# Mixing sum of the recurrent projections on GpSimd, value copies on ScalarE, one buffer for two 32-row results

## The chip, the cores and the metric

One core of a Trainium2 chip runs the whole kernel. The metric is the device time of one execution in microseconds (us), the median of several runs. TensorE (PE in the profile) multiplies matrices; VectorE (DVE), ScalarE (ACT) and GpSimd (POOL) do the elementwise work; SyncE (SP) issues the loads and stores. Each engine works through its own instructions strictly in order, and waits where one of them needs something that another engine or a transfer has not finished.

## What is computed

One layer of a hybrid decoder, for 256 prompt tokens and 8 decode tokens, so 264 columns in all:

```python
x = x + 0.5 * swiglu(rmsnorm(x, n1), f1g, f1u, f1d)          # first FFN, width 5504
proj = rmsnorm(x, nm) @ w_in                                 # q, k, v of attention | recurrent columns
xm = proj + mu * (prev - proj)                               # recurrent part: mix with the token before
r, k, v, wl, al, gl = split(xm)                              # 1024 + 1024 + 1024 + 64 + 64 + 128
S, y = wkv_scan(S0, r, logw, k, v, kk, a)                    # RWKV-7 state, 16 heads of 64
mixed = concat(attention, groupnorm(y) * g)
x = x + mixed @ w_out
x = x + 0.5 * swiglu(rmsnorm(x, n2), f2g, f2u, f2d)          # second FFN
y = rmsnorm(x, final)
```

All of it is float32. The change touches the line `xm = ...` and the scan over the prompt, which the kernel computes in chunks of 64 tokens with the inverse of a triangular matrix for each chunk.

## The kernel before

**The weight stream.** Activations lie with the model dimension on the 128 partitions and the 264 tokens along the free axis. Every weight matrix is streamed once, in chunks of 128x512. `chunk` (L116 to L129) loads a chunk into the ring `raw` (6 buffers, SP), rounds it on ScalarE to `hi` (L127, ring of 4), and forms the remainder `lo = raw - hi` on VectorE (L58 through the helper `tt`; some chunks on GpSimd). `gemm` (L133) then multiplies each of the four 128x128 blocks three times, hi by the rounded activation, hi by its remainder and lo by the rounded activation: 12 matmuls a chunk, into the accumulators `acc`. A cast or a subtraction that is late stops TensorE when the chunks ahead of it are used up.

**The mixing stage.** Between the FFNs stand 38 column blocks of w_in (4 chunks each). `win` computes one. `shifted` (L400) handles the 26 recurrent ones: block 0 and 1 are the small inputs `la` and `sgl`, then r, k and v of each of 8 pairs of heads. VectorE scales the accumulator by the norm into `pj` (a ring of three, raised in priority), GpSimd saves the last columns, ScalarE writes the previous token's columns times mu into `d`, and VectorE adds the own columns times `nmu` (that is 1 - mu) with one scalar_tensor_tensor (the helper `stt`, L61).

**The recurrent pairs.** `prep` (L419) makes the decay and key matrices of a pair (with a reciprocal of 128x264 on VectorE, L439). Two pairs form a batch, 4 batches in all. `chain` (L550) works on a batch: it loads the triangular matrices from DRAM into `X` and `Xt` (L562, L563), runs 30 steps of two small VectorE instructions each (`st`, then `Xt`, L569 to L576), sends the result through DRAM into `TT` (L581, L586), transposes the 32x32 blocks on VectorE into `TN` (L591), and multiplies twice on TensorE for the off-diagonal blocks, with a ScalarE copy `zs` between (L610). `TN` uses 32 of each 64 partitions, `zs` the other 32. Then come `pW` and `pU` on TensorE, the copies `W` (L637) and `uv` (L638 on VectorE, L639 on ScalarE), the products with W (pP, pG), those with uv (pN, pY), and the chunk-by-chunk state products.

**What sets the order.** All of these are generators, advanced one step after each weight chunk. The framework's scheduler then places every instruction of each engine by a simulated timeline in which data and buffers are waited for, with `chunk` and `pj` raised in priority. So a change of one instruction's engine can move others.

Of the kernel before, what the change touches and what calls it, by code (L numbers as in the profile page):

```python
# [9 lines left out]
AF = mybir.ActivationFunctionType  # L10
ALU = mybir.AluOpType
AX = mybir.AxisListType

P = 128
NP = 256
NB = 8
T = NP + NB
# [7 lines left out]
HALF = (slice(0, 64), slice(64, 128))  # L25
# [22 lines left out]
def body(tc, I, O):  # L48
    nc = tc.nc
    V, A, G, TE, SP = nc.vector, nc.scalar, nc.gpsimd, nc.tensor, nc.sync  # L50
    cnt = [0]

    def uid(s):
        cnt[0] += 1
        return f"{s}{cnt[0]}"

    def tt(e, out, a, b, op):
        return e.tensor_tensor(out=out, in0=a, in1=b, op=op)  # L58

    def stt(out, a, s, b, op0, op1):  # L60
        return V.scalar_tensor_tensor(out=out, in0=a, scalar=s, in1=b, op0=op0, op1=op1)  # L61
# [5 lines left out]
    def act(out, in_, f, **k):  # L67
        return A.activation(out=out, in_=in_, func=f, **k)  # L68
# [18 lines left out]
    def spawn(g):  # L87
        tasks.append(g)
        return g
# [5 lines left out]
    with ExitStack() as ctx:  # L95
# [17 lines left out]
        def mp():  # L113
            return pp.tile([P, 512], F32, tag="m", bufs=NM, name=uid("m"))
# [49 lines left out]
        def vc(i):  # L164
            return vec[:, i:i + 1]
# [192 lines left out]
        def mixing_body(mx, n2, n3, XD):  # L358
            def fix(shape, name):
                return mx.tile(list(shape), F32, name=name)  # L360

            def ring(shape, tag, bufs):
                return mx.tile(list(shape), F32, tag=tag, bufs=bufs, name=uid(tag))
# [16 lines left out]
            nmu = fix((P, NSH), "nmu")  # L380
# [11 lines left out]
            def win(t):  # L392
                ps = acc()
                gemm(ps, I["win"][t], n2.xs, tick, share=t >= LKV + 4)
                if not have[0]:
                    n2.rstd(rs)
                    have[0] = True
                return ps

            def shifted(t, d):  # L400
                ps = win(t)
                pj = PJ[t % 3]
                with tc.high_priority():
                    tt(V, pj[:, 1:1 + T], ps[:, :T], rs, ALU.mult)
                G.tensor_copy(shc[:, t, :], pj[:, NP:NP + NB + 1])
                act(d[:, :NP], pj[:, 0:NP], AF.Copy, scale=vc(VMU + t))
                A.copy(d[:, NP:], ss[:, t, :])
                stt(d, pj[:, 1:1 + T], nmu[:, t:t + 1], d, ALU.mult, ALU.add)
                return d

            la, sgl = fix((P, T), "la"), fix((P, T), "sgl")
# [138 lines left out]
            def chain(bt):  # L550
                n = bt.n
# [17 lines left out]
                for s in range(1, 31):  # L569
                    m, w = -(-s // ng), 31 - s  # L570
                    t = ring((ng * nr, m, w), "st", 2)
# [5 lines left out]
                for g in range(ng):  # L577
                    d = Y[g * nr:(g + 1) * nr].rearrange("p j t -> p (j t)")
# [10 lines left out]
                TN = ring((P, n * 4, 32), "TN", 1)  # L589
# [3 lines left out]
                def sub(h, x):  # L593
                    return slice(h * 64 + x * 32, h * 64 + x * 32 + 32)

                def quads(k):
                    return slice(k * 4, k * 4 + 4), slice(k * P, k * P + P)

                ps = mp()
                for c in range(4):  # L600
                    for k in range(n):
                        for h in range(2):
                            j = k * 4 + c
                            mm(ps[sub(h, 1 - k), j * 32:j * 32 + 32],
                               bt.Gm[k][h][sub(h, 0), c, 32:64], TN[sub(h, 0), j, :])
                zs = ring((P, n * 4, 32), "zs", 1)
                for k in range(n):
                    c, x = quads(k)
                    for h in range(2):
# [8 lines left out]
                for k in range(n):  # L618
                    c, x = quads(k)
# [4 lines left out]
                uv = bt.UV  # L624
                W, PT = ring((P, n, 3, 64), "W", 1), ring((P, n, 3, 64), "PT", 1)
                N = ring((P, n, 4, 64), "N", 1)
                pW, pU = mp(), mp()
# [7 lines left out]
                                       bt.KR[k][HALF[h], a, c, :])  # L635
                pW, pU = (ps.rearrange("p (k c t) -> p k c t", k=n, c=4) for ps in (pW, pU))
                A.copy(W, pW[:, :, 1:4, :])  # L637
                V.tensor_copy(uv[HALF[0], :, :, HALF[0]].rearrange("p c k t -> p k c t"), pU[HALF[1]])  # L638
                A.copy(uv[HALF[1], :, :, HALF[1]].rearrange("p c k t -> p k c t"), pU[HALF[0]])  # L639
                yield  # L640
                pP, pG = mp(), mp()
                for k in range(n):
# [62 lines left out]
                for k in range(n):  # L705
                    p, o = bt.p0 + k, Ys[k]
# [116 lines left out]
            def dec_attend(p, qs):  # L823
# [44 lines left out]
                for i, q in enumerate(qs):  # L868
                    G.tensor_copy(q[:, NP:T], od[:, i])

            shifted(0, la)
            act(tw[0:64, :], la[0:64, :], AF.Tanh)
            shifted(1, sgl)
            act(sgl, sgl, AF.Sigmoid)
            bat, att, bts, qs = [], [], [], []
            for kind, i in SEQ:
                if kind == "b":
                    bt = newbatch(i)
                    for k in range(BATCH[i]):
                        p = bt.p0 + k  # L880
                        x = [shifted(2 + 3 * p + j, tmp()) for j in range(3)]
                        spawn(prep(p, bt, k, *x))
                    bat.append(spawn(chain(bt)))
                    bts.append(bt)
                    if len(bat) == len(BATCH):
                        A.dma_start(O["sh"], shc)
                elif kind == "kv":
                    w, p = i // 2, i % 2
# [6 lines left out]
                else:  # L895
# [6 lines left out]
                    if i % 4 == 3:  # L902
                        p = i // 4
                        d = spawn(dec_attend(p, qs[4 * p:]))
# [187 lines left out]
```

## Time and profile before

| | us |
|---|---|
| median of 3 runs | 2003.16 |
| the 3 runs | 2001.62, 2003.16, 2003.61 |
| the profiled execution's own time | 2001.57 |
| its span in the profile | 1999.8 |
| busy: TensorE / VectorE / ScalarE / GpSimd | 1969.5 / 1301.4 / 1065.4 / 343.1 |
| VectorE / ScalarE / GpSimd busy in the recurrent part, 690 to 1190 us | 369.2 / 327.3 / 146.1 |

The span runs from the first to the last instruction of the profiled execution; 1.77 us lie around it. Busy time of an engine that nobody waits for costs nothing. A row of the timeline gives the start, the duration, the engine, the line (L58, L61, L68 and L74 are the helpers `tt`, `stt`, `act` and `mm`), the operation, output and input by name, and in brackets the idle time before it with what ended it.

### The profile page before, as it was taken

The page shows a single profiled execution, that of the slowest core. Times are in us where ns is not written, and L with a number is a line of the kernel's source. Part 1 is how long each engine was busy: PE and PEld are TensorE (multiplying, and loading weights), DVE is VectorE, ACT ScalarE, POOL GpSimd, SP SyncE. Part 2 cuts the span into 40 slices and gives each one's busy share as a digit, 9 for nine tenths or more (in the row PEclk, how much of TensorE's full clock was granted, in tenths as well). Part 3 has the DMA queues.
Part 4 walks back from the last instruction along what each step waited for, and adds up shares of the span by engine and source line. Part 5 has one row for each costly group of instructions (what it writes and reads, how often), then busy time and mean ns, then how long its engine had stood idle before and what let it go on. Part 6 is the DMA issues. An engine that isn't in the chain of part 4 may idle for free.

```text
span 1999.8 us, 45897 instructions
## 1 busy us (share of the span) xinstructions
PE 1969.5 (98%) x17212; PEld 1933.6 (97%) x17212; DVE 1301.4 (65%) x2546; ACT 1065.4 (53%) x2137; POOL 343.1 (17%) x437
## 2 busy tenths in 40 slices
PE   9999999999999999998998999999999999999998
PEld 9999999999999999997987899999999999999997
DVE  5865555655556577687867676765666666666665
ACT  5644444444444456775666765654444444444445
POOL 0401001010010121121124553120101001010012
PEclk9999999999999999999999999999999999999999
DMA  7666666655556667554555546565666666666654
GB/s 230 178 190 194 185 192 191 184 184 176 187 178 184 181 196 222 160 148 121 155 144 148 162 144 196 174 181 178 187 190 192 181 190 194 184 192 183 195 179 146
DMA packets 229232, 358.77 MB, mean 179 GB/s; under 512 B 42616, under 2 KB 84240, under 8 KB 229008
## 3 DMA queue, kind: packets, MB, share of 16 engines
q1 hardware_dynamic: 223120, 349.72, 57.9%
q10 hardware_dynamic: 5888, 6.11, 1.0%
q8 instruction: 135, 2.21, 0.4%
q14 instruction: 89, 0.73, 0.1%
HBM read 347.59 MB, written 10.22 MB: 179 GB/s over the span
## 4 chain that ended last, share of the span: by engine, by line
PE 91%; DVE 4%; DMA 2%; ACT 1%; issue 1%; SPq 1%; POOL 0%; ACTq 0%; DVEq 0%; POOLq 0%
PE acc L74 84%; PE m L74 6%; DVE lo L58 1%; DMA raw<-in_gu 1%; DVE st L58 1%; DVE Xt L58 1%; DMA raw<-in_win 0%; ACT t L68 0%; ACT hi L127 0%; DMA sb<-Xt 0%; DMA TT<-sb 0%; DVE y L58 0%; SPq L562 0%; DMA Xt<-sa 0%; SPq L563 0%
## 5 line engine op out<-in xcount | busy, mean ns | idle before, releaser
L127 ACT CAST hi<-raw 128x512 fp32r<-128x512 f32 (+2 forms) x1304 | 778.5, 601 | 818.0 <-PE acc L74 725.1
L58 DVE TENSOR_TENSOR lo<-raw,hi 128x512 fp32r<-128x512 f32 (+1 forms) x1248 | 854.4, 688 | 535.8 <-ACT hi L127 512.0
L74 PE MATMUL acc<-s,hi 128*128 128x264 f32 x5940 | 1111.7, 286 | 1.1 <-ACT hi L127 1.1
L74 PEld LDWEIGHTS acc<-s,hi 128*128 128x128 f32 x5940 | 923.3, 188 | 8.4 <-ACT hi L127 1.8
L74 PE MATMUL acc<-s,lo 128*128 128x264 f32 x2970 | 848.2, 286 | 4.9 <-DVE lo L58 4.6
L74 PEld LDWEIGHTS acc<-s,lo 128*128 128x128 f32 x2970 | 558.4, 188 | 9.5 <-DVE lo L58 6.4
L74 PE MATMUL acc<-t,hi 128*128 128x264 f32 x2752 | 502.8, 284 | 0.0
L74 PEld LDWEIGHTS acc<-t,hi 128*128 128x128 f32 x2752 | 425.9, 188 | 0.0
L74 PE MATMUL acc<-t,lo 128*128 128x264 f32 x1376 | 388.5, 284 | 0.0
L58 POOL TENSOR_TENSOR t<-t,t 128x264 f32<-128x264 f32 (+1 forms) x148 | 150.8, 1019 | 1148.6 <-ACT hi L127 789.9
L74 PEld LDWEIGHTS acc<-t,lo 128*128 128x128 f32 x1376 | 258.1, 188 | 0.1
L74 PE MATMUL acc<-y,hi 128*128 128x264 f32 x648 | 123.9, 284 | 0.0
L74 PEld LDWEIGHTS acc<-y,hi 128*128 128x128 f32 x648 | 101.2, 188 | 0.2
L74 PE MATMUL acc<-y,lo 128*128 128x264 f32 x324 | 91.3, 282 | 0.0
L58 DVE TENSOR_TENSOR t<-acc,t 128x264 f32<-128x264 f32 x156 | 67.4, 432 | 35.9 <-PE acc L74 35.7
L58 POOL TENSOR_TENSOR lo<-raw,hi 128x512 fp32r<-128x512 f32 x56 | 75.4, 1347 | 63.3 <-ACT hi L127 36.9
L58 POOL TENSOR_TENSOR o<-o,o 128x264 f32<-128x264 f32 x43 | 36.5, 848 | 187.4 <-ACT o L68 181.7
L74 PE MATMUL acc<-o,hi 128*128 128x264 f32 x324 | 62.4, 282 | 0.0
L74 PEld LDWEIGHTS acc<-y,lo 128*128 128x128 f32 x324 | 60.9, 188 | 0.0
L61 DVE SCALAR_TENSOR_TENSOR s<-acc,s 128x264 f32<-128x264 f32 x96 | 40.6, 428 | 15.9 <-PE acc L74 15.5
L74 PEld LDWEIGHTS acc<-o,hi 128*128 128x128 f32 x324 | 50.0, 188 | 0.0
L74 PE MATMUL m<-s,hi 128*128 128x264 f32 x260 | 48.1, 285 | 0.0
(252 smaller groups left out, 1336.9 us busy)
## 6 DMA issues: line engine op xcount, KB each, us to landing
raw<-in_gu SPq DMA_DIRECT2D x688, 256.0 KB, 3.4
raw<-in_dn SPq DMA_DIRECT2D x224, 256.0 KB, 2.9
raw<-in_win SPq DMA_DIRECT2D x152, 256.0 KB, 3.5
raw<-in_dn SPq DMA_DIRECT2D x160, 192.0 KB, 2.7
raw<-in_wout SPq DMA_DIRECT2D x48, 256.0 KB, 3.3
raw<-in_wout SPq DMA_DIRECT2D x32, 128.0 KB, 3.1
s<-xsp SPq DMA_DIRECT2D x16, 132.0 KB, 3.9
ld<-in_sT SPq DMA_DIRECT2D x16, 128.0 KB, 3.6
```

Source lines behind the costliest of these rows:

```text
L58: return e.tensor_tensor(out=out, in0=a, in1=b, op=op)
L61: return V.scalar_tensor_tensor(out=out, in0=a, scalar=s, in1=b, op0=op0, op1=op1)
L74: TE.matmul(out, lhsT, rhs, start=start, stop=stop, **k)
L127: A.copy(hi[:, :w], raw[:, :w])
```

## The change

```diff
@@ shifted
                 act(d[:, :NP], pj[:, 0:NP], AF.Copy, scale=vc(VMU + t))
                 A.copy(d[:, NP:], ss[:, t, :])
-                stt(d, pj[:, 1:1 + T], nmu[:, t:t + 1], d, ALU.mult, ALU.add)
+                if t < 2:
+                    stt(d, pj[:, 1:1 + T], nmu[:, t:t + 1], d, ALU.mult, ALU.add)
+                    return d
+                own = ring((P, T), "own", 1)
+                act(own, pj[:, 1:1 + T], AF.Copy, scale=nmu[:, t:t + 1])
+                tt(G, d, d, own, ALU.add)
                 return d
@@ chain
-                zs = ring((P, n * 4, 32), "zs", 1)
+                zs = TN
@@ chain
                 A.copy(W, pW[:, :, 1:4, :])
-                V.tensor_copy(uv[HALF[0], :, :, HALF[0]].rearrange("p c k t -> p k c t"), pU[HALF[1]])
-                A.copy(uv[HALF[1], :, :, HALF[1]].rearrange("p c k t -> p k c t"), pU[HALF[0]])
+                for h in range(2):
+                    A.copy(uv[HALF[h], :, :, HALF[h]].rearrange("p c k t -> p k c t"), pU[HALF[1 - h]])
```

The own columns of r, k and v are scaled on ScalarE into `own`, a ring with a single buffer, and GpSimd adds them to `d`: 24 times. Both `uv` copies of a batch are on ScalarE. `zs` lies in the unused partitions of `TN`; its separate buffer of 1024 bytes a partition is gone; `own` takes 1056. The lines of the changed kernel are 5 higher from L413 on. In the order of the program the change shows as follows.

ScalarE at the copies `W` and `uv` of batch 0; first before, then with the change (`t`, `own`: the two scalings of the v block of pair 5; `kr`, `BT`: copies for the next batch's pairs).

```order
L68 ACTIVATE t_12855<-pj_10571,vec 128x256
L637 COPY W_12986<-m_12989 128x384
L516 COPY kr_12737<-m_13028 64x2x64 x4
L523 COPY BT_13040<-m_13035 128x4x64
L525 COPY BT_13040<-m_13035 64x4x64
L639 COPY uv_10754<-m_12990 64x2x4x64
```

```order
L68 ACTIVATE t_12889<-pj_10571,vec 128x256
L68 ACTIVATE own_13183<-pj_10571,nmu 128x264
L642 COPY W_13019<-m_13022 128x384
L644 COPY uv_10754<-m_13023 64x2x4x64 x2
L521 COPY kr_12769<-m_13061 64x2x64 x4
```

A scaling now stands ahead of `W`, and both `uv` copies follow it directly; before, six copies for the next batch stood between `W` and ScalarE's `uv` copy.

VectorE around the reciprocal of pair 4 (pairs and batches are counted from 0), `pj` of the r block of pair 5 and the first inverse step of batch 1 (`st`), before and with the change.

```order
L58 TENSOR_TENSOR lo_12780<-raw_12778,hi_12779 128x512
L439 RECIPROCAL t_12635<-m_12674 128x264
L61 SCALAR_TENSOR_TENSOR kr_12737<-t_12634,t_12680 128x256
L58 TENSOR_TENSOR pj_10572<-acc_12603,rs 128x264
L58 TENSOR_TENSOR kr_12737<-t_12147,t_12680 128x256
L58 TENSOR_TENSOR lo_12798<-raw_12796,hi_12797 128x512
L61 SCALAR_TENSOR_TENSOR t_12635<-t_12635,t_12634 128x264
L58 TENSOR_TENSOR lo_12859<-raw_12857,hi_12858 128x512
L58 TENSOR_TENSOR st_12817<-X_12584,Xt_12585 128x30
L58 TENSOR_TENSOR t_12635<-t_12635,t_12631 128x264
L58 TENSOR_TENSOR lo_12919<-raw_12917,hi_12918 128x512
```

```order
L444 RECIPROCAL t_12665<-m_12704 128x264
L61 SCALAR_TENSOR_TENSOR kr_12769<-t_12664,t_12710 128x256
L58 TENSOR_TENSOR pj_10572<-acc_12633,rs 128x264
L58 TENSOR_TENSOR kr_12769<-t_12171,t_12710 128x256
L58 TENSOR_TENSOR lo_12830<-raw_12828,hi_12829 128x512
L61 SCALAR_TENSOR_TENSOR t_12665<-t_12665,t_12664 128x264
L58 TENSOR_TENSOR st_12849<-X_12612,Xt_12613 128x30
L58 TENSOR_TENSOR lo_12893<-raw_12891,hi_12892 128x512
L58 TENSOR_TENSOR t_12665<-t_12665,t_12661 128x264
L58 TENSOR_TENSOR Xt_12613<-Xt_12613,st_12849 128x30
L58 TENSOR_TENSOR lo_12952<-raw_12950,hi_12951 128x512
```

Two subtractions stood between the reciprocal and `st` (`lo_12798`, `lo_12859`), now one (`lo_12830`): the second has moved behind `st`. ScalarE at the same place, with the change: the scaling `own` of pair 5 stands between the copies of values and the next cast.

```order
L127 CAST hi_12829<-raw_12828 128x512
L127 CAST hi_12892<-raw_12891 128x512
L479 COPY uv_12170<-m_12785 64x2x64 x2
L68 ACTIVATE own_12745<-pj_10572,nmu 128x264
L479 COPY uv_12170<-m_12785 64x2x64 x2
L127 CAST hi_12951<-raw_12950 128x512
```

VectorE at the first inverse step of batch 2, before and with the change (the reciprocal is that of pair 6, `pj` is that of the k block of pair 7).

```order
L58 TENSOR_TENSOR lo_14056<-raw_14054,hi_14055 128x512
L58 TENSOR_TENSOR pj_10570<-acc_13805,rs 128x264
L58 TENSOR_TENSOR lo_14147<-raw_14145,hi_14146 128x512
L58 TENSOR_TENSOR st_13905<-X_13672,Xt_13673 128x30
L439 RECIPROCAL t_13723<-m_13762 128x264
```

```order
L58 TENSOR_TENSOR lo_14100<-raw_14098,hi_14099 128x512
L58 TENSOR_TENSOR st_13948<-X_13711,Xt_13712 128x30
L444 RECIPROCAL t_13764<-m_13803 128x264
L58 TENSOR_TENSOR Xt_13712<-Xt_13712,st_13948 128x30
L61 SCALAR_TENSOR_TENSOR kr_13868<-t_13763,t_13809 128x256
L58 TENSOR_TENSOR kr_13868<-t_13187,t_13809 128x256
L58 TENSOR_TENSOR pj_10570<-acc_13848,rs 128x264
L61 SCALAR_TENSOR_TENSOR t_13764<-t_13764,t_13763 128x264
L58 TENSOR_TENSOR st_13951<-X_13711,Xt_13712 128x29
L58 TENSOR_TENSOR lo_14191<-raw_14189,hi_14190 128x512
```

Here too `st` and the reciprocal have moved ahead of one subtraction (`lo_14147` before, `lo_14191` now), and ahead of `pj`.

## The prediction

> **What bounds the kernel now.** I read the page first: its span, the busy engines, and the chain that ended last.
>
> ```profile
> span 1999.8 us, 45897 instructions
> PE 1969.5 (98%) x17212; PEld 1933.6 (97%) x17212; DVE 1301.4 (65%) x2546; ACT 1065.4 (53%) x2137; POOL 343.1 (17%) x437
> PE 91%; DVE 4%; DMA 2%; ACT 1%; issue 1%; SPq 1%; POOL 0%; ACTq 0%; DVEq 0%; POOLq 0%
> ```
>
> TensorE is busy for 98% of the span and holds 91% of the chain. The change leaves every matmul in place, so it can only move the stops of TensorE. The windows say where these lie. The columns are the window, its length, busy time and instruction count of PE, PEld, DVE, ACT and POOL, the granted clock, the DMA share and GB/s; the sum is over six windows from 690 to 1190 us, in which the recurrent part lies.
>
> ```profile
> 300.00:400.00 100.00, 100.00 (x822) 100.00 (x822) 57.69 (x101) 46.76 (x83) 8.67 (x8) 1.00 0.61 187
> 850.00:930.00 80.00, 73.03 (x858) 67.75 (x858) 68.49 (x215) 50.71 (x133) 18.43 (x38) 0.96 0.52 142
> sum 500.00, PE 481.94 PEld 448.97 DVE 369.19 ACT 327.33 POOL 146.07; mean PE 80.32 PEld 74.83 DVE 61.53 ACT 54.55 POOL 24.35
> ```
>
> In the first FFN (300 to 400 us) TensorE never stops. It needs 100/822 = 0.1217 us a matmul there, so a chunk's 12 take 1.46 us; I use that figure below. In the recurrent part it stops for 500 - 481.94 = 18.1 us. That is the most that can be gained: 0.9% of the time. The list of TensorE's waits in the same 500 us names what ends these stops (us in total, times, longest).
>
> ```profile
> PE acc L74 <- DVE lo L58: 4.6, 4, 1.8
> PE m L74 <- ACT W L637: 3.2, 2, 2.1
> PE m L74 <- DVE st L58: 3.1, 2, 2.4
> PE m L74 <- ACT t L68: 3.1, 3, 1.7
> PE m L74 <- ACT uv L639: 2.2, 2, 2.0
> ```
>
> So 7.7 us end on VectorE (4.6 + 3.1), and 8.5 on ScalarE (3.2 + 3.1 + 2.2). The change relieves the first engine and loads the second.
>
> **The change part by part.** Durations first, from the groups of 690 to 1190 us with shapes kept apart (count, busy us, mean ns of one, idle time before).
>
> ```profile
> L61 DVE SCALAR_TENSOR_TENSOR t<-pj,nmu,t 128x264 f32<-128x264 f32 x24 | 11.5, 483 | 0.6 <-ACT t L68 0.6
> L638 DVE COPY uv<-m 64x512 f32<-64x512 f32 x4 | 2.8, 693 | 0.5 <-PE m L74 0.4
> L639 ACT COPY uv<-m 64x512 f32<-64x512 f32 x4 | 2.3, 578 | 2.9 <-DVE uv L638 2.9
> L68 ACT ACTIVATE t<-t,vec 128x264 f32<-128x264 f32 x8 | 4.1, 513 | 0.0
> L58 POOL TENSOR_TENSOR o<-o,o 128x264 f32<-128x264 f32 x15 | 11.7, 780 | 40.5 <-ACT o L68 40.5
> L58 POOL TENSOR_TENSOR t<-t,t 128x264 f32<-128x264 f32 x2 | 2.5, 1264 | 17.8 <-ACT hi L127 17.8
> ```
>
> VectorE loses 24 x 0.483 + 4 x 0.693 = 11.6 + 2.8 = 14.4 us. ScalarE gains 24 scalings; the trace has none from `pj` by `nmu`, and the nearest row, a scaling of the same 128x264, takes 0.513, so 12.3 us, and with 4 x 0.578 for the copies 14.6 us. GpSimd gains 24 additions at 0.780 to 1.264, 19 to 30 us on top of 146. All three have room in 500 us (369, 327 and 146 busy), so none becomes a bound by its sum. What counts is what stands ahead of the instructions for which TensorE waits.
>
> **Batch 0, `W` and `uv`.** On ScalarE, then on TensorE:
>
> ```profile
> 921.05 0.51 ACT L68 ACTIVATE t<-pj,vec 128x256 f32<-128x256 f32 x1 [4.30 <-DVE pj L58]
> 921.59 0.48 ACT L637 COPY W<-m 128x384 f32<-128x384 f32 x1
> ...
> 924.99 0.58 ACT L639 COPY uv<-m 64x512 f32<-64x512 f32 x1 [1.18 <-DVE uv L638]
> ```
>
> ```profile
> 922.12 0.45 PE L74 MATMUL m<-uv,gm 64*64 64x64 f32 x8 [1.13 <-ACT W L637]
> ...
> 925.62 0.59 PE L74 MATMUL m<-gm,W 64*64 64x64 f32 x6 [1.97 <-ACT uv L639]
> ```
>
> (The names in a matmul row are of a bundle; the bracket is what counts.) `W` is late because ScalarE stood at a scaling that waited for `pj`. With the change a second scaling stands there too: `W` comes 0.51 later, and TensorE waits 1.13 + 0.51 = 1.64. Both `uv` copies then follow `W`: it ends at 921.59 + 0.51 + 0.48 = 922.6, and they at 922.6 + 2 x 0.578 = 923.7. TensorE wanted `uv` at 925.62 - 1.97 = 923.65, now 0.51 later: no wait is left. The pair of waits goes from 3.10 to 1.64: **-1.5 us**. The copies of the next batch that go behind `uv` come 1.2 later, under the weight chunks that TensorE still has. The other `uv` wait is 2.2 - 2.0 = 0.2 and goes too: **-0.2**. The two copies in series could cost 0.578 a batch where ScalarE had been free; with 3 other batches that is +1.7 at the most, if nothing stands between. I take 0, since VectorE's copy (0.693) was no faster and `uv` waited for it.
>
> **Batch 1, `st` ahead of a subtraction.** VectorE, then TensorE:
>
> ```profile
> 899.34 1.80 DVE L439 RECIPROCAL t<-m 128x264 f32<-128x264 f32 x1
> ...
> 901.33 0.42 DVE L58 TENSOR_TENSOR pj<-acc,rs 128x264 f32<-128x264 f32 x1
> ...
> 902.96 0.68 DVE L58 TENSOR_TENSOR lo<-raw,hi 128x512 fp32r<-128x512 f32 x1
> 906.33 0.19 DVE L58 TENSOR_TENSOR st<-X,Xt 128x30 f32<-128x30 f32 x1 [2.69 <-DMA raw<-in_win]
> ...
> 906.78 0.68 DVE L58 TENSOR_TENSOR lo<-raw,hi 128x512 fp32r<-128x512 f32 x1
> ```
>
> ```profile
> 907.52 0.39 PE L74 MATMUL acc<-s,lo 128*128 128x264 f32 x1 [1.81 <-DVE lo L58]
> ```
>
> VectorE sat idle for 2.69 us ahead of `st` with the subtraction that TensorE wanted queued behind it. The idle was a transfer's (the row names a weight load that landed last; `st` reads X and Xt, loaded on the same queue). A lighter VectorE can't end this: it had nothing to do. In the changed order `st` stands one subtraction earlier, so the one that ran at 902.96 waits too. It then runs at 906.43 to 907.11, TensorE has 1.46 us of work from it, and starts the next chunk at 907.17 + 1.46 = 908.6 instead of 907.52: **+1.1 us**. On SP one weight load more stands among the loads of X and Xt, so I don't expect them earlier; came they 1.1 us earlier, this would be 0; 1.46, a whole chunk, is the other end.
>
> **Batch 2, the same with a reciprocal.** VectorE, then TensorE:
>
> ```profile
> 973.10 0.68 DVE L58 TENSOR_TENSOR lo<-raw,hi 128x512 fp32r<-128x512 f32 x1
> 976.54 0.19 DVE L58 TENSOR_TENSOR st<-X,Xt 128x30 f32<-128x30 f32 x1 [2.75 <-DMA Xt<-sa]
> 976.64 1.80 DVE L439 RECIPROCAL t<-m 128x264 f32<-128x264 f32 x1
> ...
> 979.51 0.69 DVE L58 TENSOR_TENSOR lo<-raw,hi 128x512 fp32r<-128x512 f32 x1
> ```
>
> ```profile
> 980.25 0.39 PE L74 MATMUL acc<-s,lo 128*128 128x264 f32 x1 [0.85 <-DVE lo L58]
> ```
>
> The subtraction of 973.10 now stands behind `st`, the reciprocal and `pj`: it would start 0.34 behind 979.51 (the step from one 128x264 row to the next), at 979.85, end at 980.5, and the chunk after it would start at 980.6 + 1.46 = 982.1 instead of 980.25, +1.8. On SP the weight load that stood just ahead of the last load of Xt now stands two loads earlier, so `st` may come somewhat earlier; I take **+1.4**, between 0 and 1.8, nearer the end that the rows give.
>
> **The scaling ahead of a cast, and the single buffer.** The r block of pair 5 on ScalarE:
>
> ```profile
> 898.56 1.08 ACT L474 COPY uv<-m 64x128 f32<-64x128 f32 x4
> 899.54 0.62 ACT L127 CAST hi<-raw 128x512 fp32r<-128x512 f32 x1
> ```
>
> With the change `own` stands between two of these copies, and waits for `pj` (901.33 + 0.42 = 901.75). The cast then starts at 901.75 + 0.51 + half of 1.08 = 902.8 instead of 899.54, and ends at 903.4. Its subtraction is the one of 906.78: hidden here by 3.4 us. For the last pair, k and v scalings must each wait for GpSimd's addition of the one before, since `own` has one buffer; there ScalarE's `zs` and TensorE follow:
>
> ```profile
> 987.15 1.10 ACT L610 COPY zs<-m 32x128 f32<-32x128 f32 x4
> 989.23 0.45 PE L74 MATMUL m<-TT,zs 32*32 32x32 f32 x32
> ```
>
> The margin is 989.23 - 988.25 = 0.98 us, and two additions at 1.264 make 2.5: 0 to 1.5. I take **+0.5**, nearer the margin, since ScalarE has waits of its own between them. `zs` in TN: the copies read what the products with TN wrote, so they stood behind TN's readers already: **0**.
>
> **Sum:** -1.5 - 0.2 + 1.1 + 1.4 + 0.5 = +1.3 us. The profiled execution of 2001.57 becomes 2002.9. The median shown stands 2003.16 - 2001.57 = 1.59 above that execution, so I forecast 2002.87 + 1.59 = **2004.5**. A difference within 0.2% (4 us) is about what a measurement of this kernel can't tell from no change.
>
> **The rivals.** *VectorE's relief is felt* (faster). If 14.4 us less work, spread over the part, ended all VectorE waits, 4.6 + 3.1, and the ScalarE terms of -1.5 - 0.2 stood, it would be -9.4: 1993.8; half of the VectorE waits gives -5.6, 1997.6. For it: VectorE is the busiest helper. Against: two of the four `lo` waits are shown above, and stand behind a transfer's idle and a 1.80 us reciprocal.
>
> *ScalarE is held in order* (slower). `own` waits for `pj` ahead of casts; the delay worked out above is 902.8 - 899.5 = 3.3 us. Where the slack is smaller than that, TensorE stops. The r blocks of pairs 3, 4 and 5 have such a place; three at 2.3 (a slack of 1.0, as at `zs`) give +6.9 in place of the +0.5: 2004.5 + 6.4 = 2010.9. It decides from a slack under 2 us at all three. Against: no wait of TensorE on `hi` stands in the list.
>
> *GpSimd's additions block VectorE* (slower).
>
> ```profile
> 1046.45 1.29 POOL L58 TENSOR_TENSOR lo<-raw,hi 128x512 fp32r<-128x512 f32 x1 [0.39 <-POOL bk L828]
> ...
> 1046.70 1.08 DVE L58 TENSOR_TENSOR st<-X,Xt 128x30 f32<-128x30 f32 x1 [3.66 <-DMA s<-xsp]
> ```
>
> The small `st` took 1.08 us, against 0.19 at 906.33, and ended with GpSimd's instruction at about 1047.75: it stood still for 0.89. If each of 24 additions held VectorE so, that is 21 us, more than the 14.4 relieved. At the six stops that VectorE ends it gives 6 x 0.89 = +5.3: 2009.8; it decides when an addition runs just ahead of at least five of them. [...] *The change does nothing* beyond the order: 2003.2.
>
> **How the numbers follow.** My forecast has a chance of 0.55. Its bounds are -1.5 - 0.2 = -1.7 with every cost at nothing, and -1.7 + 1.46 + 1.8 + 1.5 + 1.7 = +4.8 with every cost at its end: 2001.5 to 2008.0. Of the 0.55, 0.43 lies within 0.2%, 0.08 is slower, 0.04 faster. VectorE's relief has 0.23, held ScalarE 0.12, blocking 0.07, nothing 0.03. Faster .27, same .46, slower .27. The range takes in half of the relief, 1997.6, and the blocking at 2009.8: 1997 to 2010.5.
>
> **What would show it.** In the changed trace: VectorE's total down by 14 us, 24 ScalarE rows `own` of about 0.51, 24 GpSimd additions of 0.78 to 1.3; at batch 0 a `W` wait near 1.6 and no `uv` wait; at batch 1 and 2 waits for `lo` of some 2.5 to 3 us behind `st`. Waits on `hi` in TensorE's list would speak for the held ScalarE; `lo` or `st` rows stretched beside an `own` addition for the blocking; a sum of VectorE-ended waits under 4 us for the relief. I am wrong if the loads of X and Xt land more than 2 us earlier or later than before, or if the stops of attention, behind batch 2, are dealt anew.

## The result, and the profile after

The changed kernel takes 2015.59 us (median of 5 runs, 2013.44 to 2017.41); the kernel before 2002.45 (5 runs, 2001.51 to 2003.61). The ratio is 1.0064, 95% interval 1.0053 to 1.0075: **slower by 0.64%, 13 us**, where 2004.5 and a range up to 2010.5 had been forecast. The profiled execution took 2014.44.

The page of the changed kernel, span and busy engines:

```profile
span 2012.4 us, 45937 instructions
PE 1973.8 (98%) x17212; PEld 1938.8 (96%) x17212; DVE 1296.1 (64%) x2518; ACT 1076.8 (54%) x2165; POOL 354.8 (18%) x461
```

The span is 12.6 us longer. TensorE runs the same 17212 matmuls but is busy 1973.8 - 1969.5 = 4.3 us more, so it stood still for 8.3 us more. VectorE's busy time fell by 1301.4 - 1296.1 = 5.3 us, not by the 14 us that the prediction named as a sign: the instructions left to it took longer in all. The recurrent part (690 to 1210 us, columns as above) of the kernel before, then of the changed one:

```profile
690.00:1210.00 520.00, 501.94 (x5180) 468.97 (x5179) 384.84 (x985) 338.93 (x837) 157.96 (x247) 0.99 0.55 161
```

```profile
690.00:1210.00 520.00, 493.58 (x5075) 461.13 (x5074) 369.53 (x941) 342.99 (x850) 162.07 (x265) 0.98 0.53 156
```

All of the new idle is there: 520 - 501.94 = 18.1 us before, 520 - 493.58 = 26.4 after. TensorE's waits of the changed kernel in 690 to 1210 us (us in total, times, longest) say at what:

```profile
PE acc L74 <- DVE lo L58: 8.2, 6, 2.9
PE m L74 <- DVE st L58: 4.2, 1, 4.2
PE m L74 <- DVE S L61: 3.9, 2, 2.4
PE acc L74 <- POOL s L58: 1.8, 1, 1.8
PE m L74 <- ACT t L763: 1.6, 1, 1.6
PE m L74 <- ACT TT L626: 1.4, 2, 1.0
PE m L74 <- ACT W L642: 1.1, 1, 1.1
...
PE m L74 <- ACT kr L521: 0.6, 1, 0.6
```

The `uv` wait has gone and `W` is smaller, but `lo` has grown from 4.6 to 8.2, and state steps (`S`, L61), `TT`, `s` and the attention's `t` are new. VectorE, which was relieved, ends 8.2 + 4.2 + 3.9 = 16.3 us of the stops listed, against 7.7 in the list of before.

**Batch 0.** ScalarE, then TensorE:

```profile
925.69 0.51 ACT L68 ACTIVATE t<-pj,vec 128x256 f32<-128x256 f32 x1 [4.00 <-DVE pj L58]
926.11 0.50 ACT L68 ACTIVATE own<-pj,nmu 128x264 f32<-128x264 f32 x1
926.63 0.48 ACT L642 COPY W<-m 128x384 f32<-128x384 f32 x1
927.13 1.17 ACT L644 COPY uv<-m 64x512 f32<-64x512 f32 x2
928.33 1.07 ACT L521 COPY kr<-m 64x128 f32<-64x128 f32 x4
```

```profile
927.16 0.45 PE L74 MATMUL m<-uv,gm 64*64 64x64 f32 x8 [1.11 <-ACT W L642]
...
929.45 0.27 PE L74 MATMUL m<-gm,W 64*64 64x64 f32 x2 [0.65 <-ACT kr L521]
```

`own` stands ahead of `W` as the order said, and no `uv` wait is left. The 0.65 us is paid at `kr`, a copy for the next batch that went behind `uv`, and 0.24 us more follows at 930.61 for `BT`, another of them; I had costed these copies at nothing.

**Batch 1.** VectorE, then TensorE:

```profile
905.16 0.69 DVE L58 TENSOR_TENSOR lo<-raw,hi 128x512 fp32r<-128x512 f32 x1
905.76 0.43 DVE L61 SCALAR_TENSOR_TENSOR t<-t,t 128x264 f32<-128x264 f32 x1
909.43 0.19 DVE L58 TENSOR_TENSOR st<-X,Xt 128x30 f32<-128x30 f32 x1 [3.24 <-DMA X<-sa]
909.57 0.69 DVE L58 TENSOR_TENSOR lo<-raw,hi 128x512 fp32r<-128x512 f32 x1
```

```profile
910.31 0.59 PE L74 MATMUL acc<-s,lo 128*128 128x264 f32 x1 [2.92 <-DVE lo L58]
910.70 0.64 PE L74 MATMUL acc<-s,hi 128*128 128x264 f32 x2
...
913.33 0.41 PE L74 MATMUL acc<-s,hi 128*128 128x264 f32 x2
```

One subtraction fewer stands ahead of `st`; VectorE idles for 3.24 us on the loads, and TensorE stops for 2.92 (before 1.81). Two matmuls then take 0.64 us, and 0.41 three microseconds later: TensorE came back at a granted clock of 0.50, which holds from 909.90 to 913.31 us (below).

**Batch 2.** VectorE, then TensorE:

```profile
974.36 0.69 DVE L58 TENSOR_TENSOR lo<-raw,hi 128x512 fp32r<-128x512 f32 x1
979.06 0.19 DVE L58 TENSOR_TENSOR st<-X,Xt 128x30 f32<-128x30 f32 x1 [4.01 <-DMA Xt<-sa]
979.16 1.80 DVE L444 RECIPROCAL t<-m 128x264 f32<-128x264 f32 x1
...
982.37 1.29 DVE L58 TENSOR_TENSOR lo<-raw,hi 128x512 fp32r<-128x512 f32 x2
```

```profile
983.11 0.39 PE L74 MATMUL acc<-s,lo 128*128 128x264 f32 x1 [2.13 <-DVE lo L58]
```

2.13 us where 0.85 had been.

**The last pair, `own` with its single buffer.** ScalarE, then TensorE:

```profile
990.05 0.52 ACT L68 ACTIVATE own<-pj,nmu 128x264 f32<-128x264 f32 x1 [0.77 <-POOL t L58]
990.60 0.17 ACT L494 COPY XD<-m 128x8 f32<-128x8 f32 x1
```

```profile
990.81 0.71 PE L74 MATMUL m<-kr,bk 64*128 64x128 f32 x5 [0.39 <-ACT XD L494]
```

As foreseen, a scaling waited for GpSimd's addition of the one before (0.77 us); TensorE lost 0.39 us, at the copy `XD` that stands behind the scaling.

**The state steps `S`.** VectorE in the kernel before, then in the changed one, then TensorE there (`TN<-TT` are the transposes of the next batch's triangular blocks, which read a load):

```profile
936.28 0.47 DVE L61 SCALAR_TENSOR_TENSOR S<-m,wc,Z 128x64 f32<-128x64 f32 x2
939.27 0.43 DVE L591 STREAM_TRANSPOSE TN<-TT 32x256 f32<-32x256 f32 x1 [2.52 <-DMA TT<-sb]
```

```profile
940.20 0.43 DVE L596 STREAM_TRANSPOSE TN<-TT 32x256 f32<-32x256 f32 x1 [3.44 <-DMA TT<-sb]
...
941.83 0.43 DVE L596 STREAM_TRANSPOSE TN<-TT 32x256 f32<-32x256 f32 x1 [1.02 <-DMA TT<-sb]
...
943.24 0.47 DVE L61 SCALAR_TENSOR_TENSOR S<-m,wc,Z 128x64 f32<-128x64 f32 x2
```

```profile
943.58 0.27 PE L74 MATMUL m<-S,PT 64*64 64x64 f32 x2 [1.46 <-DVE S L61]
```

Before, this `S` had run when VectorE came to the transposes; now both transposes stand ahead of it, and it waits through their idle. The same happens at 1014 us (4.08 and 1.33 us of idle at the transposes), where TensorE stops for 2.43 us. It is the mechanism of `st`, a step that waits for a transfer with wanted work queued behind it, at places that I had not looked at.

### The profile page after: what moved, and what is told of

Read it like the earlier page. It is cut to its first block, busy times and chain, and to the rows that moved or that the text cites. A ratio compares the mean times of both kernels' runs of the same rounds, so it can differ in the third digit from the quotient of the medians.

```text
span 2012.4 us, 45937 instructions
## 1 busy us (share of the span) xinstructions
PE 1973.8 (98%) x17212; PEld 1938.8 (96%) x17212; DVE 1296.1 (64%) x2518; ACT 1076.8 (54%) x2165; POOL 354.8 (18%) x461
## 4 chain that ended last, share of the span: by engine, by line
PE 46%; DVE 4%; ACT 1%; issue 1%; DMA 1%; SPq 1%; POOL 0%; DVEq 0%; ACTq 0%; POOLq 0%
PE acc L74 43%; PE m L74 3%; DVE lo L58 1%; DVE st L58 1%; DVE Xt L58 1%; ACT t L68 0%; DMA Xt<-sa 0%; DMA TT<-sb 0%; DVE y L58 0%; ACT hi L127 0%; DMA sb<-Xt 0%; SPq L586 0%; DVE y L61 0%; DMA raw<-in_wout 0%; DVE sta L65 0%
## 5 line engine op out<-in xcount | busy, mean ns | idle before, releaser
L61 DVE SCALAR_TENSOR_TENSOR s<-acc,s 128x264 f32<-128x264 f32 x96 | 40.6, 427 | 15.9 <-PE acc L74 15.5
```

## The experiments

Four theories stood. **Order:** the scheduler, given a lighter VectorE, puts waiting steps ahead of subtractions and deals the later part anew. **Load:** the added scalings and additions delay what stands behind them, GpSimd's by blocking VectorE. **Late sums:** r, k and v come late over the longer way. **Copies:** `uv` on ScalarE. Every ratio is against the kernel before on the same chip, with its 95% interval, and is worked out from all runs, so it can differ a little from that of the two medians; idle is TensorE's in 690 to 1210 us of the profiled execution.

| kernel | median us, its before | ratio (interval) | idle us |
|---|---|---|---|
| the change | 2015.59, 2002.45 | 1.0064 (1.0053 to 1.0075) | 26.4 |
| uv_only | 2006.97, 2004.43 | 1.0013 (1.0004 to 1.0022) | 20.2 |
| sum_only | 2016.15, 2004.43 | 1.0048 (1.0034 to 1.0062) | 29.3 |
| sum_dve | 2006.32, 2004.43 | 1.0006 (0.9997 to 1.0015) | 17.4 |
| relief | 2010.70, 2004.43 | 1.0032 (1.0019 to 1.0044) | 22.8 |
| zs_only | 2004.51, 2003.71 | 1.0002 (0.9993 to 1.0011) | 18.4 |
| load_act | 2006.11, 2003.08 | 1.0013 (1.0004 to 1.0022) | 22.1 |
| load_only | 2009.70, 2003.78 | 1.0028 (1.0018 to 1.0038) | 21.1 |
| dummy | 2016.41, 2003.78 | 1.0058 (1.0046 to 1.0070) | 24.0 |
| before_redealt | 2008.29, 2003.08 | 1.0020 (1.0011 to 1.0028) | 24.6 |
| pin_as_before | 2013.83, 2003.78 | 1.0047 (1.0035 to 1.0059) | 27.9 |
| change_pin_later | 2006.84, 2003.08 | 1.0014 (1.0005 to 1.0023) | 24.2 |
| change_pin_b12 | 2007.95, 2003.71 | 1.0022 (1.0013 to 1.0031) | 24.6 |
| before_pin_later | 1999.99, 2003.78 | 0.9978 (0.9970 to 0.9987) | 18.3 |
| before_pin_again | 1999.88, 2003.71 | 0.9981 (0.9972 to 0.9989) | 17.1 |
| before_pin_all | 2004.91, 2003.08 | 1.0005 (0.9996 to 1.0014) | 20.6 |

### Which part of the change

uv_only puts the two copies of L638 and L639 on ScalarE and changes nothing else.

> Of the change, only the two uv copies on ScalarE; the mixing sum stays on VectorE and zs keeps its buffer. The order theory (taking the 24 sums off VectorE lets waiting steps move ahead of subtractions that TensorE wants) expects about the time before, 2000 to 2005 us, since VectorE keeps its 24 sums. The theory that ScalarE's copies in series make the chain late expects most of the loss of 13 us: 2010 or more. My own term for this edit was -1.7 us: 2001.

+0.13%: some loss, not the bulk; my term of -1.7 us isn't seen either. sum_only leaves the copies as they were:

```diff
-                for h in range(2):
-                    A.copy(uv[HALF[h], ...], pU[HALF[1 - h]])
+                V.tensor_copy(uv[HALF[0], ...], pU[HALF[1]])
+                A.copy(uv[HALF[1], ...], pU[HALF[0]])
```

> The mixing sum on ScalarE and GpSimd with zs in TN, the uv copies as before (one on VectorE, one on ScalarE). The order theory and the theory of a held ScalarE or GpSimd both expect the whole loss here, 2010 to 2018 us, with the stops behind st at batch 1 and 2; the copies theory expects 2003.

+0.48%: the bulk. With uv_only's 0.13 the two make 0.61, the change's 0.64. sum_dve takes the changed kernel and only gives the addition back to VectorE:

```diff
-                tt(G, d, d, own, ALU.add)
+                tt(V, d, d, own, ALU.add)
```

> As the changed kernel, but the addition of own to d is on VectorE instead of GpSimd; ScalarE still makes own, from one buffer, ahead of casts. VectorE has its 24 instructions back (about 0.43 us each). The order theory expects about the time before, 2000 to 2006 us, with st at batch 1 behind two subtractions again. A theory in which ScalarE is held by own expects it still slow, 2010 or more; one in which GpSimd's additions block VectorE or come late expects 2003 as well.

+0.06%, its interval reaching past 1. `st` of batch 1 and 2 is back behind the subtractions of before. So ScalarE's `own` ahead of casts, with one buffer, with both `uv` copies and with `zs` in TN, costs next to nothing in this order: **the engine of the addition decides**, by 0.64 - 0.06 = 0.58%. Putting it on GpSimd does two things: it relieves VectorE and it loads GpSimd. relief does the first alone:

```diff
-                act(d[:, :NP], pj[:, 0:NP], AF.Copy, scale=vc(VMU + t))
+                act(d[:, :NP], pj[:, 0:NP] if t < 2 else pj[:, 1:1 + NP], AF.Copy, scale=vc(VMU + t))
-                stt(d, pj[:, 1:1 + T], nmu[:, t:t + 1], d, ALU.mult, ALU.add)
+                if t < 2:
+                    stt(d, pj[:, 1:1 + T], nmu[:, t:t + 1], d, ALU.mult, ALU.add)
```

> The kernel before without its 24 sums for r, k and v: the own columns' term is left out (the prompt's first scaling reads the own columns instead of the previous ones, and nothing is added), so VectorE has 11.6 us less and neither ScalarE nor GpSimd has anything more. The order theory expects it slower than before, 2006 to 2014 us, with waits for subtractions behind st at batch 1 and 2 as with the change. The theories that blame ScalarE's scalings, the single buffer or GpSimd's additions expect no loss: 1996 to 2003.

Work taken away and nothing added: **+0.32%**. Its order has `st` of batch 1 behind one subtraction, like the change, and VectorE waits there with the same picture:

```profile
903.13 0.42 DVE L61 SCALAR_TENSOR_TENSOR t<-t,t 128x264 f32<-128x264 f32 x1
906.97 0.19 DVE L58 TENSOR_TENSOR st<-X,Xt 128x30 f32<-128x30 f32 x1 [3.41 <-DMA X<-sa]
907.11 0.69 DVE L58 TENSOR_TENSOR lo<-raw,hi 128x512 fp32r<-128x512 f32 x1
```

TensorE stops for 3.10 us there, and for 2.29 and 1.68 us at `S` steps behind transposes that wait for their load, as in the changed kernel. The order theory holds for this part: work taken off VectorE, with no load added, brings stops at `S` that no kernel with VectorE's order of before has over 0.8 us.

### The load at an unchanged order

load_only keeps the sum on VectorE and adds the new work as ballast:

```diff
                 stt(d, pj[:, 1:1 + T], nmu[:, t:t + 1], d, ALU.mult, ALU.add)
+                if t >= 2:
+                    own = ring((P, T), "own", 1)
+                    act(own, pj[:, 1:1 + T], AF.Copy, scale=nmu[:, t:t + 1])
+                    tt(G, own, own, own, ALU.add)
-                zs = ring((P, n * 4, 32), "zs", 1)
+                zs = TN
```

> The kernel before, with its 24 sums kept on VectorE, plus the added load alone: ScalarE makes own for r, k and v, and GpSimd adds own to itself in its single buffer; nothing reads the result, and zs lies in TN. VectorE's order stays as before (st of batch 1 behind the same subtraction). The order theory expects 2002 to 2007 us against about 2003 to 2004. The load theory (own ahead of casts, GpSimd blocking VectorE) expects a good part of the loss: 2009 or more.

VectorE's order is the same, instruction for instruction, as before: **+0.28%**, and the 2009.70 us lie where the load theory had put them. TensorE has no stop at `S` here. load_act is the same without the line `tt(G, own, own, own, ...)`, and zs_only is `zs = TN` alone.

> As load_only, without GpSimd's 24 additions: ScalarE makes own, nobody reads it; the order on VectorE, TensorE and SP is that of the kernel before. If ScalarE's scalings cost the 5.9 us of load_only, 2008 to 2010 us here; if GpSimd's additions do (they hold VectorE), 2003 to 2005. My guess is in the middle, 2005 to 2007, since the wait for W grew by 0.6 us with load_only and the waits for subtractions behind reciprocals too.

> The kernel before with zs in TN alone: the order of every engine is that of before. I expect no difference, 0.1% at most either way. If it is slower by 0.1% or more, part of what load_act and load_only lost belongs to this edit and not to ScalarE's scalings and GpSimd's additions.

zs_only is at +0.02%, as expected; load_act at +0.13%, an interval that overlaps zs_only's; GpSimd's additions raise it to 0.28. How they do it shows in VectorE's rows at a pair's second subtraction, in load_act, then in load_only, and GpSimd's in load_only:

```profile
826.27 0.68 DVE L58 TENSOR_TENSOR lo<-raw,hi 128x512 fp32r<-128x512 f32 x1
```

```profile
826.91 1.12 DVE L58 TENSOR_TENSOR lo<-raw,hi 128x512 fp32r<-128x512 f32 x1
```

```profile
826.75 0.73 POOL L58 TENSOR_TENSOR own<-own 128x264 f32<-128x264 f32 x1 [0.65 <-ACT own L68]
```

The addition runs from 826.75 to 827.48. The subtraction, issued at 826.91, takes 1.12 instead of 0.68: 0.44 longer, of the 0.57 in which both ran. VectorE's order is the same in both kernels, so its rows can be compared one by one: 14 that overlap one of the 24 additions are 0.18 to 0.46 us longer in load_only, 5.6 us together; VectorE's busy total of the part is 385.73 us against 381.63. It is the picture of the prediction's `st` of 1.08 us beside a GpSimd subtraction.

dummy adds the load and gives VectorE 24 unused instructions in place of those it lost:

```diff
                 tt(G, d, d, own, ALU.add)
+                dm = mx.tile([P, T], mybir.dt.bfloat16, tag="dm", bufs=1, name=uid("dm"))
+                stt(dm, pj[:, 1:1 + T], nmu[:, t:t + 1], own, ALU.mult, ALU.add)
```

> The changed kernel, plus 24 multiply-and-add instructions on VectorE of the shape that was taken away, whose results (own again, in bf16) nobody reads. VectorE's total is as before, and the sum still goes through ScalarE and GpSimd. The order theory expects most of the loss back, 2003 to 2008 us. If the longer way through GpSimd makes r, k and v late, or GpSimd blocks VectorE, it stays at 2011 or more.

A miss for the order theory in its simple form: +0.58%, though VectorE's total was restored. The order of before was not: TensorE stops for `XD` (1.35 and 1.84 us) and for `S` (2.40 and 2.34 us) where before it did not. The first `st` of batch 1 and 2 even stands two and one subtractions later than before, so an early place of `st` isn't what costs here; both `S` stops are again behind transposes (5.48 and 5.10 us of idle). Late sums could explain the rest of the loss as well; this kernel doesn't tell.

### The order without the load

before_redealt changes no instruction, only pauses: `DWAIT = (8, 9, 9, 8)`.

> The kernel before with the pauses of batch 1 and 2 one weight chunk longer: no instruction added, taken away or moved to another engine, but the scheduler deals the order anew from batch 2's chain on. If what the change lost in its later part is the luck of the order, a new deal without any cause should also cost some us: 2005 to 2009. If loss needs the change's load or relief, it stays at 2002 to 2004.

**+0.20%** with no work added or moved. The two `st` stand behind the same subtractions as before, so it is the later order that costs. The longer pauses are themselves a part of that order, so this isn't shown to be chance alone. Then the reverse: hold `st` in place. In the pinned kernels `chunk` lists VectorE's subtractions, and the first `st` of a batch is issued behind the last of them, after a pause DW1 of its own (framework's `issue_after`: an order on one engine, no wait):

```diff
+DW1, BACK = (8, 11, 14, 8), (0, 1, 1, 0)
-                tt(e, lo[:, :w], raw[:, :w], hi[:, :w].bitcast(F32), ALU.subtract)
+                i = tt(e, lo[:, :w], raw[:, :w], hi[:, :w].bitcast(F32), ALU.subtract)
+                if e is V:
+                    los.append(i)
-                yield from pause(DWAIT[bt.i])
+                yield from pause(DW1[bt.i])
-                    tt(V, t, bc(X[:, s:s + 1, s + 1:], shp), bc(Y[:, :m, s:s + 1], shp), ALU.mult)
+                    back = BACK[bt.i] if s == 1 else 0
+                    with tc.issue_after(los[-back].ins) if back else nullcontext():
+                        tt(V, t, bc(X[:, s:s + 1, s + 1:], shp), bc(Y[:, :m, s:s + 1], shp), ALU.mult)
```

pin_as_before is the changed kernel with pauses (8, 9, 12, 8), which puts the two `st` where they stood before.

> The changed kernel with the first inverse step st of batch 1 and 2 held behind the subtraction behind which each stood before (one later than the change's own order); all else is left to the scheduler. If these two places are the cause, their waits fall from 2.9 and 2.1 us to about 1.8 and 0.9 and the half clock behind the first goes: 2009 to 2011 us. If the loss is spread over later stops it stays at 2013 to 2017.

+0.47%, under the change's 0.64, though the intervals touch: TensorE's stops at the two places fall from 2.92 and 2.13 us to 1.78 and none, but they are a small part of the loss, and the idle (27.9 us) has moved to later stops, 3.69 us of it to an `S` behind transposes at 1014 us. before_pin_later is the kernel before with the line of the diff above, two subtractions later:

> The kernel before with st of batch 1 and 2 held two subtractions later than it stood, so that the loads of X and Xt have about 2.9 us more. If VectorE's idle ahead of st is what makes these subtractions late, the waits of 1.8 and 0.85 us go, and the time falls by 2 to 4 us: 1999 to 2002. If the order there is not a lever, it stays within 1 us of before.

**-0.22%**, the fastest kernel of the study, and -0.19% when it was run again. VectorE's rows there:

```profile
905.88 0.68 DVE L59 TENSOR_TENSOR lo<-raw,hi 128x512 fp32r<-128x512 f32 x1
907.13 0.19 DVE L59 TENSOR_TENSOR st<-X,Xt 128x30 f32<-128x30 f32 x1 [0.57 <-DMA raw<-in_win]
```

The idle ahead of `st` is 0.57 us instead of 2.69, and the stop of TensorE behind it is gone: the window around it shows 10 us of 10 busy. That the gain comes from this is not shown: the idle of the whole part is 18.3 and 17.1 us in the two runs against 18.1 before, since other stops have come, among them 2.0 us for a cast at 1051 us.

```profile
905.00:915.00 10.00, 10.00 (x164) 9.16 (x163) 9.26 (x33) 7.20 (x23) 3.73 (x5) 1.00 0.75 225
```

With all four batches held back there are two more kernels, with pauses (10, 12, 15, 10) and BACK (1, 1, 1, 1): the kernel before and the changed one.

> The kernel before with the first st of all four batches held back likewise. Each idle of VectorE ahead of st that made a subtraction late is then covered: 1997 to 2001 us, 1 to 2 us under the pinned kernel of two batches, if the place is the lever also in batch 0 and 3; if the deal of the later order decides, anything from 1998 to 2008.

> The changed kernel with the first st of all four batches held back by two to four subtractions. If VectorE's idle ahead of st is a large part of the loss, it comes down to 2006 to 2010 us; if the loss is spread over the later stops, it stays above 2011.

The first is at +0.05%: more of the same was no better, so a later `st` is no gain by itself. The second is at +0.14%: of the change's 13 us, about 10 went when only the order was changed. Last, change and before with the same pins, on one chip:

> The changed kernel with st of batch 1 and 2 held where before_pin_later holds them, so that VectorE's order in this part is nearly the same in both. If the load (6 us at a like order) is the part of the loss that stays, it lies 4 to 8 us above before_pin_again: 2004 to 2008. If order is the whole of it, it comes within 2 us of before_pin_again: 1999 to 2002.

> The kernel of before_pin_later once more, as the partner on the same chip: 0.1% to 0.3% faster than before, 1998 to 2001 us.

1.0022 against 0.9981: the changed kernel costs 0.41%, 8 us, where `st` of batch 1 and 2 stands behind the same subtractions. This isn't the price of the load alone, for the rest of the order still differs: one `S` stands behind both transposes again (4.40 and 2.49 us of idle), and TensorE stops for it.

```profile
942.86 0.37 PE L75 MATMUL m<-S,PT 64*64 64x64 f32 x2 [3.84 <-DVE S L62]
```

In before_pin_again no stop at `S` is over 0.8 us. With the other pins (1.0014 against 1.0005) the change costs 0.09%, and those two intervals overlap. So what the changed work costs depends on the order that it meets. No run held the transposes in place.

## Why the prediction was wrong

**The places that were argued came out near the forecast, in part by luck.** Prediction and trace of the changed kernel, in us of TensorE's stops:

| step | forecast | measured |
|---|---|---|
| batch 0, `W` and `uv` | 3.10 to 1.64 | 3.10 to 1.11 + 0.65 + 0.24 = 2.00 |
| batch 2, `uv` | -0.2 | no such wait |
| batch 1, `st` ahead of a subtraction | +1.1 | 2.92 - 1.81 = +1.1 |
| batch 2, the same with a reciprocal | +1.4 | 2.13 - 0.85 = +1.3 |
| `own` ahead of casts, single buffer | +0.5 | no wait on `hi` in the list; +0.4 at `XD` |

The sum of these is +1.5 us where +1.3 was forecast. But the stop of batch 1 is no proof of the new order, because it varies by as much where VectorE's order is that of before: 1.71 us in load_only, 2.50 in zs_only and 3.14 in load_act, with 2.58, 3.38 and 4.01 us of idle ahead of `st` as its loads landed sooner or later. At batch 2 those three show 1.41, 0.61 and 1.05, and the change's 2.13 stands clear of them. The cost of `own`, 0.508 against 0.513 us taken, and of an addition, 0.840 on the mean between 0.780 and 1.264, were right too:

```profile
L58 POOL TENSOR_TENSOR t<-t,own 128x264 f32<-128x264 f32 x24 | 20.1, 840 | 7.7 <-ACT own L68 6.0 <-ACT t L407 1.0 <-DMA raw<-in_win 0.4
...
L68 ACT ACTIVATE own<-pj,nmu 128x264 f32<-128x264 f32 x24 | 12.2, 508 | 12.6 <-DVE pj L58 9.5 <-POOL t L58 3.1
```

**The step that failed is the sum as a whole**: I added up the places that I had looked at and let the rest of the recurrent part stand as before, at a price of nothing. Of 8.4 us of new idle, 6.9 (net of old stops that went) lie elsewhere. The largest part is 3.9 us at `S`, behind transposes that wait for their load; others are at `st` (one stop of 4.2 us in the last batch, where before had two of 3.1 together), `TT`, `s` and the attention's `t`. The text named such a new deal for the attention alone ("if the stops of attention, behind batch 2, are dealt anew") and gave it no price and no chance, although the 18 us of stops that I had counted as given are themselves a product of that order. before_redealt gives a size for it: 4 us with no work added or moved.

**The rival of GpSimd blocking VectorE was real, and I gave it 0.07.** At an unchanged order on VectorE the whole load costs 0.28%, 5.9 us between the medians (load_only), of which the additions are about half: 0.28 - 0.13 = 0.15%, 3 us. The intervals of these two kernels touch at their ends, so the split is less sure than the sum. Nobody reads what these additions write in load_only, so busy time whose result nobody reads was not free here. GpSimd's own subtractions, which both kernels have, block VectorE likewise: ahead of the 4.2 us stop at `st`, between 1059 and 1068 us, three of the small steps took 1.33, 1.21 and 1.29 us, and ended 0.08 to 0.09 us behind GpSimd subtractions of 1.28, 1.28 and 1.26 us that were issued just ahead of them. Before, ahead of the stop of 2.35 us there, two steps took 0.81 and 0.76; most of the others around them take about 0.2.

**The rival of a held ScalarE fell** (sum_dve). **That VectorE's relief would be felt as a gain fell**, and with its sign: alone it costs 0.32%. The reading that fits relief's trace is that a busy VectorE had kept the scheduler from putting `st` and the transposes early, and that each of them that is early waits for a load with wanted work queued behind it; no run of relief with these steps held in place was made to prove it.

**What stays open.** Relief 0.32, load 0.28 and copies 0.13 make 0.73 against the change's 0.64; this is no exact split, since relief and copies each have an order of their own, and the changed kernel's distance to the one before went from 0.09% to 0.41% with the pins. Whether late sums add to it wasn't tried by itself. Of dummy's +0.58%, the two `S` stops of 4.7 us are one part; the rest isn't settled. The changed work in exactly the order of before wasn't tried; change_pin_b12 is the nearest.

## What to carry to other kernels

Where a scheduler sets the order from a simulated timeline, moving work off an engine is two changes: the load and a new deal of the order. Price the second from how much stop time the stretch holds, and widen the range by it; a deal without any work added or moved cost 4 us of 2003 here. Look in the trace for the step that waits for a transfer (3.24 us of idle at `st` of batch 1, and a stop of 2.92 at the subtraction behind it): what stands behind it can matter more than the engine's total. Holding one such step back by two places, in two batches, gave 0.2% (in all four batches nothing), where taking 11.6 us off the engine cost 0.3%.

## What the runs showed of the hardware

**Some stops are paid for twice.** Beside them the granted clock (column PEclk) stands at a half. Three windows of the changed kernel: the stop of batch 1, then seven microseconds with 0.39 us of idle, then the seven after them:

```profile
905.00:915.00 10.00, 6.64 (x41) 6.22 (x41) 6.76 (x18) 5.13 (x14) 3.49 (x7) 0.83 0.59 155
...
984.00:991.00 7.00, 6.61 (x107) 5.99 (x107) 6.93 (x19) 5.73 (x16) 5.78 (x8) 1.00 0.65 185
991.00:998.00 7.00, 7.00 (x65) 6.56 (x65) 6.55 (x28) 3.40 (x11) 0.98 (x2) 0.56 0.50 146
```

```profile
992.52 0.64 PE L74 MATMUL acc<-s,hi 128*128 128x264 f32 x2
```

From 991 to 998 TensorE is busy for all 7 us, but at a clock of 0.56, and a pair of 128x264 matmuls takes 0.64 us against 0.41 at full clock (913.33 above). What precedes is a run of small matmuls (64x2, 32x32 and 64x128) with a stop of 0.39 us in it. The stretch from 905 to 915 us in the kernel before, then in zs_only, whose order is the same on every engine:

```profile
905.00:915.00 10.00, 8.07 (x146) 6.70 (x145) 8.57 (x30) 6.25 (x19) 3.28 (x5) 1.00 0.55 163
```

```profile
905.00:915.00 10.00, 7.50 (x76) 6.71 (x79) 6.62 (x19) 3.87 (x10) 3.27 (x5) 0.83 0.56 142
```

One execution kept the full clock there (1.00) and the other did not (0.83); their spans are 1999.8 and 2005.4 us with 18.1 and 18.4 us of idle. So the clock's part of a single profile is partly chance, and the 4.3 us of extra busy time of the changed kernel can't be laid to the change: zs_only's TensorE is busy for 1974.0 us. In the changed kernel the clock stands at 0.50 from 909.90 to 913.31 us and from 991.82 to 998.65, for 3.41 and 6.83 us, and in the kernel before from 924.30 to 931.13, for 6.83. The first of these begins within the stop of 2.92 us that ends at 910.31, the third within the one of 1.97 us that ends at 925.62; the second begins 1.01 us behind the stop of 0.39 us that ends at 990.81. Behind the stop of 2.13 us that ends at 983.11 the clock was 1.00 up to 991 us, so the length of a stop alone doesn't tell, and what does was not shown.
